# Two units of seven products for q and k of the first half in the input projection of an encoder layer

## The chip, the cores and the metric

The kernel runs on one core of one Trainium2 chip. The metric is the time of one execution on the device in microseconds (us), the median of several runs. A core has TensorE (matrix products, called PE in the profile, its weight loads PEld), VectorE (DVE), ScalarE (ACT), GpSimd (POOL) and SyncE (SP, which here only issues DMAs). Each of them works through its own instructions in the order in which they were written and waits for the others by semaphores.

## The reference

The reference is one layer of an encoder over 256 tokens of width 2048: an input projection, attention and a recurrent block side by side, an output projection, a dense feed-forward part and a gated embedding, each with norms. Only the start is touched here:

```python
hn = rms_norm(h, g_mix_pre[i])
u = hn @ w_in[i]
q, k, v, xr, yg = jnp.split(
    u, [D_ATTN, 2 * D_ATTN, 3 * D_ATTN, 3 * D_ATTN + D_REC], axis=-1)
attn = neighborhood_attention(
    q.reshape(B, S, N_ATTN_HEADS, HEAD_DIM),
    k.reshape(B, S, N_ATTN_HEADS, HEAD_DIM),
    v.reshape(B, S, N_ATTN_HEADS, HEAD_DIM), rpb[i])
rec = rglru_bidirectional(xr, conv_w[i], conv_b[i], w_rg_a[i], b_rg_a[i],
                          w_rg_i[i], b_rg_i[i], lam[i]) * jax.nn.gelu(yg)
```

`w_in` is 2048 x 5120 in float32: q, k, v, x (`xr`) and gate (`yg`) of 1024 columns each.

## The kernel before

**Precision.** Every float32 operand is split into a high part, rounded by ScalarE's cast, and a low part, the difference that VectorE takes. A product is three matmuls, high by high, low by high and high by low, added up in PSUM.

**Tiles.** The feature matrix `hT` has 16 blocks of 128 features by 256 tokens. A weight tile holds two feature blocks (a row-block pair, `[P, 2, N]`, 512 KB) by 512 columns. It is loaded by SP into one of four buffers `wr` (L612), cast to `wh` (L700), its low part goes to `wl` (L716), each with four buffers. Its products (L758) are 2 blocks x 2 halves of the tokens x 3 = 12 matmuls of 512 columns. A chunk is 512 columns: eight tiles, added up in two PSUM banks. There are eight banks: four `acc`, which the chunks use, and four `sm` for small work such as transposes, gate products and scores.

**Order.** A `Plan` runs while the program is written. It holds a clock for each engine and a model of durations, takes the segments of products in order as the main line of TensorE, and puts the side work (generators that yield what they need) between them by readiness and lateness. What it writes is a fixed order for each engine. On the chip an engine waits where its next instruction isn't ready.

**The input projection** runs its ten chunks in the order `x0 v0 q0 k0 x1 q1 k1 v1 g0 g1` (L1493). x0 and v0 take turns tile by tile, all but the last two of each (`turns`, `apart=2`), then come q0's eight tiles, k0's eight and so on. So tiles 0 to 13 are x0's and v0's in turns with x0's last two, 14 and 15 v0's last two, 16 to 23 q0's, 24 to 31 k0's.

**What lies beside it.** While the first tiles are multiplied, `xT` is loaded and turned into the high and low parts of `hT` (L331, L333), block by block. The rows of `x` are loaded a second time as `xn` (L965) ahead of tiles 10 to 13; ScalarE squares them (L995) and the norm `rstd_x` comes from the sums. A chunk's accumulators are scaled by `rstd_x` when they are evacuated (L1112, or L1411 and L1415 for v). x's evacuation starts the transposes, the convolution and the recurrent units (`rec_unit`), q's and k's a turn of blocks by VectorE (L353) and by small DMAs through the single tiles `ev` and `sq`.

**Units of seven.** The feed-forward part and the last gate already multiply some row-block pairs in another way. With two chunks side by side, a row-block pair is a 2 x 2 problem: two token halves, two feature blocks, two column blocks. Seven products of sums and differences do for eight. `Group` holds two such chunks. `four_products` makes four of the seven, the first into empty accumulators, `made_of_four` turns these into the running sums (two copies by ScalarE, four steps by VectorE on PSUM), and `two_products` and `one_product` add the other three onto these sums. The weights for it are swapped between the two tiles on the host (`SWAPPED`), so that the sums `Q0+Q1`, `Q0+Q1+R1` and `Q1+R1` are three adds (L641, L643, L647); the last operand is the second one plus a block that GpSimd's queue adds by an accumulating DMA (`added`, L669). The features need four sums and differences for each pair, made by `sums_of` (L869, L876) and split like any operand.

Of the kernel before, what the change touches and what calls it, by code (L numbers as in the profile page):

```python
# [44 lines left out]
PLE_KS = (0, 2)  # L45
BEGIN = (6, 7)
# [5 lines left out]
def seven_ks(f):  # L52
# [13 lines left out]
    (lambda c: (("w_ple_gate", c), ("w_ple_gate", c + 1)), (2,), PLE_KS),  # L66
]
# [187 lines left out]
def layer(ctx: ExitStack, tc: tile.TileContext, a: dict, out: bass.AP):  # L255
# [211 lines left out]
    class Group:  # L467
# [23 lines left out]
        def two(self, j):  # L491
            i = len(tiles)
            tiles.append(None)
            self.twos[j] = i
            lower[self.own[j] + 1] = -1
            segs.append((two_products, self, j, i))
# [77 lines left out]
    def load_stream():  # L574
        for i, tl in enumerate(tiles):
# [3 lines left out]
            w, k, n0 = tl  # L579
            if min(fours) <= i < i_ple:  # L580
                if i in lower:
                    yield (ev_spilled, ev_half_spilled, ev_unmerged)[(0, 0, 1, 2, 2)[lower[i]]]
                yield dma(ISSUE, take=raw_kind(i))
                t = lower_tile(lower[i]) if i in lower else raw_tile(i)
                nc.sync.dma_start(t, a[w][n0 // N, k // 2])
                plan.now += COST["landing"]
                if i in ev_load:
                    loaded[i] = t
                    done(ev_load[i])
                else:  # L590
                    raws[i] = t
                    done(ev_raw[i, 2])
                continue
# [27 lines left out]
    def sum_stream():  # L621

        for i in sorted(fours):
# [26 lines left out]
            done(ev_raw[two, 2])  # L650

# [54 lines left out]
    def lo_stream():  # L706
        last_one = max(f[1] for f in ffn_fours().values())
        for i in range(len(tiles)):
# [16 lines left out]
            if i in fours:  # L725
                plan.add(last_sum(i), plan.now, -2 * SOON)

# [74 lines left out]
    def made_of_four(group):  # L802
# [49 lines left out]
    def sums_of(lhs, kx, hi, lo):  # L852
# [7 lines left out]
        kind = "mid" if lhs is hP or kx == 6 else "T4"  # L860
        for j in range(2):
            h, l = lhs.at[kx + j]
            yield dve(S, take=None if j else kind)
            if not j and kind == "mid":
# [107 lines left out]
    for i in range(2 * NT):  # L972
        extra_loads.setdefault((10 + i, 0), []).append(load_xn(i))
# [75 lines left out]

    def open_p1():  # L1050
        t1["hs"], t1["rec_hi"] = big(0, "hs", F32), big(1, "rec_hi")
# [14 lines left out]
        for n in ("qh", "ql", "kh", "kl"):  # L1066
            t1[n] = p1.tile([P, HB, S], F32R, name=n)
        for n in ("vh", "vl"):
            t1[n] = p1.tile([P, NT, N], F32R, name=n)
        t1["pp"] = p1.tile([P, 2, NT, 2, KEYS], F32R, name="pp")  # L1070
# [6 lines left out]
        nc.gpsimd.memset(ssr, 0.0)  # L1077

# [20 lines left out]
    def second_tiles():  # L1099
        plan.reach(ev_x)  # L1100
        t1["rec_lo"], t1["attnT"] = big(2, "rec_lo"), big(3, "attnT", F32)
        mixT.blocks(t1["rec_hi"], t1["rec_lo"], 8, NB)
# [392 lines left out]
    first = []  # L1495
    for n, c in enumerate(ORDER.split()):
        (n0, post), half = CHUNKS[c[0]], int(c[1])
        ch = Chunk(post(half), (open_p1, second_tiles)[n] if n < 2 else None)
        if n < 2:
            first.append((ch, "w_in", n0 + half * N))  # L1500
# [751 lines left out]
    for i in range(min(fours), max(f[1] for f in fours.values() if f[4] is hF.ev_sums)):  # L2252
        if i % (W_BUFS + MORE_W) < MORE_W:
            more_w[i] = i % (W_BUFS + MORE_W)
    places = list(RING)
    for n, i in enumerate(sorted(lower)):
        lower[i] = next(j for j in places if j < 3 or n < len(lower) - 4)
        places.remove(lower[i])
        places.append(lower[i])
    first_slot = {i: n % 2 for n, i in enumerate(sorted(fours))}  # L2260
# [27 lines left out]
    soonest = min(fours)  # L2288
    plan.add(load_stream(), late=lambda: (
# [8 lines left out]
    plan.add(norm_x())  # L2298
    plan.add(decay(), 30.0)
# [108 lines left out]
```

## Time and profile before

| | |
|---|---|
| median of 3 runs | 1139.56 us (1138.49 to 1139.64) |
| the profiled execution | 1138.81 us |
| its span, first to last instruction | 1137.0 us |
| mean granted TensorE clock | 0.998 |
| TensorE matmuls | 5140 |
| DMA | 269.54 MB, 237 GB/s on average |

The profile is one execution. Its views name engine, source line, operation and the tiles `out<-in`; a group's row gives busy time, the mean of one instruction in ns, and the engine's idle time just before with what ended it. In timelines the first two numbers are the start and the duration in us. A matmul's own duration overlaps with that of its neighbours, since they are pipelined; the distance from one start to the next is what it costs.

### The profile page before, as it was taken

To read this page: it belongs to the slowest core of one execution; us is meant where nothing else is said; L and a number is where in the kernel's file an instruction comes from. 1 tells how busy PE (TensorE), PEld (TensorE's weight loads), DVE (VectorE), ACT (ScalarE), POOL (GpSimd) and SP (SyncE) were. 2 spreads that over 40 slices of the span, in tenths; PEclk is the share of its full clock that TensorE was granted. 3 is DMA by queue.
4 is the path that set the end of the run, shared out by engine and by line. 5 is a ranking of instruction groups with operands and counts; after the bars stand their busy time and mean duration, and the time that the engine had idled before them with its cause. 6 is when DMAs were issued, how large, how long until landed. Compare 5 with 4: busy or idle time off the path is not lost.

```text
span 1137.0 us, 15223 instructions
## 1 busy us (share of the span) xinstructions
PE 1127.5 (99%) x5140; PEld 938.2 (83%) x5140; DVE 962.1 (85%) x1250; ACT 741.0 (65%) x994; POOL 154.5 (14%) x245
## 2 busy tenths in 40 slices
PE   9999999999999999999999999999999999999997
PEld 8888888888888888888888888888888888888886
DVE  6768787788469998899998889999989988888986
ACT  6776788876448566566566656666565664676674
POOL 0000000000000032232011043132121223200200
PEclk9999999999999999999999999999999999999999
DMA  8867566565686986887887777897887788967862
GB/s 311 303 193 219 173 183 187 166 201 181 206 302 184 344 254 226 234 259 222 277 285 232 240 222 216 249 269 235 271 275 280 233 242 255 305 208 271 269 198 101
DMA packets 110686, 269.54 MB, mean 237 GB/s; under 512 B 36432, under 2 KB 42576, under 8 KB 109200
## 3 DMA queue, kind: packets, MB, share of 16 engines
q1 hardware_dynamic: 95568, 242.60, 64.0%
q0 software_dynamic: 14752, 25.84, 11.1%
q8 instruction: 40, 0.66, 0.2%
q14 instruction: 38, 0.31, 0.1%
q10 hardware_dynamic: 288, 0.14, 0.0%
HBM read 250.70 MB, written 9.44 MB: 229 GB/s over the span
## 4 chain that ended last, share of the span: by engine, by line
PE 96%; DVE 1%; ACT 1%; DMA 1%; issue 0%; SPq 0%; DVEq 0%; POOL 0%; ACTq 0%; POOLq 0%
PE acc L758 69%; PE acc L769 8%; PE acc L768 8%; PE acc L767 8%; PE tr L344 1%; DVE wl L716 0%; DMA sq<-ev 0%; PE half L2119 0%; PE acc L2119 0%; PE warm L2305 0%; PE pg L391 0%; PE pg L392 0%; PE pg L393 0%; ACT wh L700 0%; PE po L1435 0%
## 5 line engine op out<-in xcount | busy, mean ns | idle before, releaser
L716 DVE TENSOR_TENSOR wl<-wr,wh 128x1024 fp32r<-128x1024 f32 (+1 forms) x295 | 352.9, 1210 | 77.8 <-ACT wh L700 72.4
L700 ACT CAST wh<-wr 128x1024 fp32r<-128x1024 f32 (+1 forms) x295 | 304.9, 1042 | 136.8 <-PE acc L758 84.2
L758 PE MATMUL acc<-wh,hT_mix_hi 128*128 128x512 f32 x376 | 146.6, 390 | 0.0
L758 PE MATMUL acc<-wh,hT_mix_lo 128*128 128x512 f32 x376 | 146.3, 389 | 0.0
L758 PE MATMUL acc<-wl,hT_mix_hi 128*128 128x512 f32 x376 | 146.3, 389 | 0.0
L700 ACT CAST wh<-ple 128x1024 fp32r<-128x1024 f32 (+1 forms) x75 | 76.0, 1018 | 82.2 <-DVE ple L643 54.6
L363 POOL DMA_DIRECT2D mT<-mid x164 | 96.8, 636 | 238.3 <-DVE mid L353 117.6
L758 PE MATMUL acc<-wl,hT_hi 128*128 128x512 f32 x320 | 124.6, 390 | 0.0
L758 PE MATMUL acc<-wh,hT_hi 128*128 128x512 f32 x316 | 124.5, 394 | 0.0
L758 PE MATMUL acc<-wh,hT_lo 128*128 128x512 f32 x316 | 123.2, 390 | 0.0
L669 POOL DMA_DIRECT2D ple<-in_w_ffn_up x32 | 28.7, 897 | 539.7 <-DVE ple L643 386.3
L716 DVE TENSOR_TENSOR wl<-ple,wh 128x1024 fp32r<-128x1024 f32 (+1 forms) x75 | 88.0, 1177 | 9.3 <-ACT wh L700 9.3
L758 PEld LDWEIGHTS acc<-wl,hT_mix_hi 128*128 128x128 f32 x376 | 70.6, 188 | 14.7 <-DVE wl L716 0.2
L758 PEld LDWEIGHTS acc<-wh,hT_mix_hi 128*128 128x128 f32 x376 | 70.6, 188 | 14.6
L758 PEld LDWEIGHTS acc<-wh,hT_mix_lo 128*128 128x128 f32 x376 | 70.6, 188 | 14.6
L758 PEld LDWEIGHTS acc<-wl,hT_hi 128*128 128x128 f32 x320 | 60.1, 188 | 13.1 <-DVE wl L716 0.2
L758 PEld LDWEIGHTS acc<-wh,hT_lo 128*128 128x128 f32 x316 | 59.4, 188 | 11.6
L758 PEld LDWEIGHTS acc<-wh,hT_hi 128*128 128x128 f32 x316 | 59.4, 188 | 11.4
L758 PE MATMUL acc<-w,hT_mix_hi 128*128 128x512 f32 x144 | 47.3, 389 | 0.0
L716 DVE TENSOR_TENSOR wl<-lower,wh 128x1024 fp32r<-128x1024 f32 x35 | 42.4, 1215 | 3.1 <-ACT wh L700 3.1
L700 ACT CAST wh<-lower 128x1024 fp32r<-128x1024 f32 x35 | 36.6, 1052 | 10.7 <-PE acc L758 6.8
L758 PE MATMUL acc<-wh,hT_ffn_hi 128*128 128x512 f32 x96 | 37.8, 393 | 0.4 <-ACT hT_ffn_hi L331 0.4
(472 smaller groups left out, 2536.6 us busy)
## 6 DMA issues: line engine op xcount, KB each, us to landing
wr<-in_w_in SPq DMA_DIRECT2D x77, 512.0 KB, 4.5
wr<-in_w_ffn_gate SPq DMA_DIRECT2D x70, 512.0 KB, 5.6
wr<-in_w_ffn_down SPq DMA_DIRECT2D x54, 512.0 KB, 6.0
wr<-in_w_ffn_up SPq DMA_DIRECT2D x50, 512.0 KB, 5.0
wr<-in_w_out SPq DMA_DIRECT2D x32, 512.0 KB, 4.4
wr<-in_w_ple_gate SPq DMA_DIRECT2D x30, 512.0 KB, 4.7
lower<-in_w_ffn_up SPq DMA_DIRECT2D x27, 512.0 KB, 6.4
third<-in_w_ffn_gate SPq DMA_DIRECT2D x18, 512.0 KB, 5.7
```

The source lines that it names most:

```text
L344: nc.tensor.transpose(tr[:, b, t * P : (t + 1) * P], e[:, t, sl], ident)
L363: (nc.gpsimd if i in pool else nc.sync).dma_start(dst[32 * j : 32 * j + 32, :, :, i, :], src[32 * i : 32 * i + 32, :, :, j, :],)
L669: nc.gpsimd.dma_start(dst, src, accum_op=ALU.add)
L700: nc.scalar.copy(his[i][:, 0 : src.shape[1], :] if n == 2 else his[i][:, j, :], src)
L716: nc.vector.tensor_tensor(out=los[i][:, m, :], in0=src, in1=f32(his[i][:, m, :]), op=ALU.subtract)
L758: nc.tensor.matmul(accs[t], x[:, sl], w[:, j, :], start=st and m == 0, stop=sp and m == 2, **group)
L767: nc.tensor.matmul(dst, x[0], wh, start=start, stop=False, skip_group_check=seeded)
L768: nc.tensor.matmul(dst, x[1], wh, start=False, stop=False, skip_group_check=seeded)
L769: nc.tensor.matmul(dst, x[0], wl, start=False, stop=stop, skip_group_check=seeded)
```

## The change

q0 and k0 become a `Group` side by side. The row-block pairs 0 and 2 of both (`IN_KS`) are units of seven, the other six pairs stay ordinary tiles. The four products of the first unit stand before the sixth turn of x0 and v0, those of the second after it (`IN_AT`). Then come the last two tiles of x0 and of v0, a pair of q and k tiles, two products of the first unit, a pair, the other three products of both units, and then the last four tiles of q0 and of k0 (`apart=4`).

By tiles: 10 and 11 are the four products of the first unit, 12 and 13 x0 and v0, 14 and 15 the four products of the second unit, 16 and 17 x0's last, 18 and 19 v0's last, 20 and 21 a pair of q and k, 22 two products, 23 and 24 a pair, 25 to 27 two, one and one product, 28 to 31 q0's last, 32 to 35 k0's last.

x0 and v0 get `sm` banks, so that q0 and k0 can have all four `acc` banks at once. The sums of the weights go into tiles of the later q, k, probability and `sq` buffers, the feature sums into `at0`, a new tile `sums_more` and v's buffer; these buffers are opened for their own use later (`open_v`, `open_qk`). `in_sums` makes the feature sums, `in_sum_stream` the weight sums, `in_last_sum` the accumulating load. The loads of `xn` move from ahead of tiles 10 to 13 to ahead of tiles 17 to 20 of the new order.

```diff
+IN_KS = (0, 2)
+IN_AT = (5, 6)
...
+    (lambda c: (("w_in", c), ("w_in", c + 2)), (0,), IN_KS),
...
+            if i in in_load:
+                for kb, f in extra_loads.get((i, 0), ()):
+                    yield dma(kb)
+                    f()
+                j, second = in_load[i]
+                yield dma(512, take=None if second else "wr")
+                loaded[i] = in_rows[j] if second else raw_tile(i)
+                nc.sync.dma_start(loaded[i], a[w][n0 // N, k // 2])
+                done(ev_load[i])
+                continue
...
+    def in_sum_stream():
+
+        for j, i in enumerate(into.own):
+            yield ev_load[i]
+            yield ev_load[i + 1]
+            Q, R, both = loaded.pop(i), loaded.pop(i + 1), in_both[j]
+            yield dve(3 * N)
+            nc.vector.tensor_tensor(out=both[:, 0, :], in0=Q[:, 0, :], in1=Q[:, 1, :], op=ALU.add)
+            nc.vector.tensor_tensor(out=both[:, 1, :], in0=both[:, 0, :], in1=R[:, 1, :], op=ALU.add)
+            nc.vector.tensor_tensor(out=Q[:, 1, :], in0=Q[:, 1, :], in1=R[:, 1, :], op=ALU.add)
+            raws[i] = both
...
+    def in_last_sum(j):
+        late, last = into.last[j][:2]
+        there = Event()
+        yield from added(in_both[j][:, 1, :], late[:, 0, :], there)
+        yield there
+        raws[last] = in_both[j][:, 1:2, :]
+        done(ev_raw[last, 2])
...
+    def in_sums():
+        more = t1["pool"].tile([P, 2, N], F32R, name="sums_more")
+        pairs = [[x.rearrange("p k s -> p (k s)") for x in at0], (more[:, 0, :], more[:, 1, :])]
...
+            p = pairs[n]
+            yield from sums_of(hT, kx, *p, t1["here"])
...
-        yield ev_rf
-        yield act(N)
-        u, v = (t2["pool"].tile([P, N], F32, tag="junk", name="u", bufs=2) for _ in range(2))
+        if group.lhs is hT:
+            u, v = (t1["ig"][:, n, :, :].rearrange("p c s -> p (c s)") for n in range(2))
+            yield act(N)
...
-        extra_loads.setdefault((10 + i, 0), []).append(load_xn(i))
+        extra_loads.setdefault((17 + i, 0), []).append(load_xn(i))
...
-        ch = Chunk(post(half), (open_p1, second_tiles)[n] if n < 2 else None)
...
-            turns(first, hT, KS, apart=2)
-        elif n > 1:
-            seg(ch, "w_in", n0 + half * N, hT, KS, after=start_biases if n == 3 else None)
+        ch = Chunk(post(half), {0: open_hs, 1: open_v, 2: open_qk, 3: second_tiles}.get(n), slot="sm" if n < 2 else "acc")
...
+            into = Group([made_of[m] for m in ORDER.split()[2:4]], hT, KS, IN_KS, apart=4)
+            into.own, into.twos, into.last = [], {}, {}
+            m = len(KS) - 2
+            for i, k in enumerate(KS[:m]):
+                for j, b in enumerate(IN_AT):
+                    if i == b:
+                        into.four(j)
+                for d, w, o in first:
+                    seg(d, w, o, hT, [k], i == 0, False)
+            for j, b in enumerate(IN_AT):
+                if b >= m:
+                    into.four(j)
+            for d, w, o in first:
+                seg(d, w, o, hT, KS[m:], first=False)
+            steps = list(('0', '1ab'))
+            m = len(into.rest) - into.apart
+            for i in range(m):
+                into.pair(i)
...
+            for d, w, o in into.chunks if into.apart else ():
+                seg(d, w, o, hT, into.rest[m:], first=False)
+        elif n > 3:
+            seg(*made_of[c], hT, KS)
...
+    plan.add(in_sums(), 17.0, late=-LATE)
+    plan.add(in_sum_stream(), late=-LATE)
```

More of the change, by code (lines that the diff above doesn't have):

```diff
@@ L726, in lo_stream @@
                 plan.add(last_sum(i), plan.now, -2 * SOON)
+            if i in into.own:
+                plan.add(in_last_sum(into.own.index(i)), plan.now)
     MM = 0.2263
@@ L850, in one_product, with sums_of @@
         spent(i)
[L852 removed]
+    def sums_of(lhs, kx, hi, lo, here=None):
         lhs.sums[kx] = {
@@ L859, in sums_of @@
         yield lhs.ev[kx + 1]
-        kind = "mid" if lhs is hP or kx == 6 else "T4"
+        kind = None if here is not None else "mid" if lhs is hP or kx == 6 else "T4"
         for j in range(2):
@@ L863, in sums_of @@
             yield dve(S, take=None if j else kind)
-            if not j and kind == "mid":
+            if not j and not kind:
+                e, f = here[:, 0, :], here[:, 1, :]
+            elif not j and kind == "mid":
                 at_ = mid_tile()
@@ L2259, in layer @@
         places.append(lower[i])
+    in_load = {i + n: (j, n) for j, i in enumerate(into.own) for n in range(2)}
+    for i in in_load:
+        ev_load[i] = Event()
+    for j, i in enumerate(into.own):
+        gives[i] = gives[into.twos[j]] = gives[into.last[j][1]] = "x"
     first_slot = {i: n % 2 for n, i in enumerate(sorted(fours))}
```

61 lines of the change are left out of this document (49 added, 12 removed).

## The prediction

> **What bounds the kernel now.** I began with the page: busy times, then the chain of work that ended last.
>
> ```profile
> span 1137.0 us, 15223 instructions
> PE 1127.5 (99%) x5140; PEld 938.2 (83%) x5140; DVE 962.1 (85%) x1250; ACT 741.0 (65%) x994; POOL 154.5 (14%) x245
> ...
> PE 96%; DVE 1%; ACT 1%; DMA 1%; issue 0%; SPq 0%; DVEq 0%; POOL 0%; ACTq 0%; POOLq 0%
> ```
>
> The chain runs through TensorE for 96% of the span. The view of waits says how much of the rest is TensorE standing still; these are all its rows for the whole kernel.
>
> ```profile
> PE final L2206 <- ACT diag L2204: 2.5, 1, 2.5
> PE warm L2305 <- POOL ones L309: 1.1, 1, 1.1
> PE acc L758 <- ACT hT_ffn_hi L331: 0.4, 1, 0.4
> PE sc L391 <- DVE pp L327: 0.3, 1, 0.3
> ```
>
> That is 4.3 us in all, and only the 0.3 lies in the input projection. So time is won by issuing fewer matmuls and lost by any new wait. The chain in order of time gives the price of a matmul (start, us, what):
>
> ```profile
> 8.22 39.98 PE acc L758 x176
> ...
> 71.10 29.05 PE acc L758 x128
> ```
> ```profile
> 388.28 0.23 PE acc L767
> ...
> 393.78 0.23 PE acc L758
> ```
>
> 39.98/176 = 0.2272 us in an ordinary tile of the head, 29.05/128 = 0.2270 later. In the units of seven that the FFN already has, 24 matmuls lie between 388.28 and 393.78: 0.229 each. The 0.39 us that a single matmul shows elsewhere is its length in the pipeline and isn't used.
>
> The Trainium skill (Perfetto Trace Analysis, Identifying the Most-Contended Engine) calls matmul busy time a bad measure and judges TensorE by the busy share of its weight loads, here 83%. Read so, 17% would be free and six pairs fewer would give 1.13 us, 6 x the mean weight load of the row below. The gapless stretch above speaks for 0.2272 each: 0.188/0.227 is 83% too, so that share is what a full TensorE shows here.
>
> ```profile
> L758 PEld LDWEIGHTS acc<-wh,hT_hi 128*128 128x128 f32 x316 | 59.4, 188 | 11.4
> ```
>
> **What the change removes.** One row-block pair of q0 and k0 takes two tiles now: 2 tiles x 2 row blocks x 2 token tiles x 3 splits = 24 matmuls. As a unit of seven it takes 7 x 3 = 21. Two units: 6 matmuls, 6 x 0.2272 = **1.36 us** off TensorE, 0.12% of the span. Nothing else on TensorE changes in number.
>
> **What it adds, and when it is due.** The head is where the answer lies. Stages of 10 us (PE, PEld, DVE, ACT, POOL busy, clock, DMA share, GB/s):
>
> ```profile
> 10.00:20.00 10.00, 10.00 (x46) 8.13 (x45) 8.26 (x12) 6.92 (x11) 0.00 (x0) 1.00 0.98 370
> 20.00:30.00 10.00, 10.00 (x46) 8.29 (x45) 6.93 (x12) 7.74 (x13) 0.00 (x0) 1.00 0.96 344
> 30.00:40.00 10.00, 10.00 (x46) 8.29 (x45) 5.23 (x7) 8.67 (x13) 0.00 (x0) 1.00 0.93 349
> 40.00:50.00 10.00, 10.00 (x48) 8.28 (x47) 8.78 (x28) 8.29 (x12) 0.00 (x0) 1.00 0.84 274
> 50.00:60.00 10.00, 10.00 (x48) 8.25 (x47) 8.88 (x18) 6.97 (x10) 0.00 (x0) 1.00 0.58 170
> 60.00:70.00 10.00, 10.00 (x54) 8.57 (x53) 6.16 (x7) 6.02 (x8) 0.00 (x0) 1.00 0.75 227
> 70.00:80.00 10.00, 10.00 (x50) 8.45 (x49) 6.61 (x7) 8.64 (x14) 0.00 (x0) 1.00 0.66 202
> 80.00:90.00 10.00, 10.00 (x45) 8.26 (x44) 6.00 (x8) 8.81 (x14) 0.00 (x0) 1.00 0.78 218
> 90.00:100.00 10.00, 10.00 (x46) 8.27 (x45) 9.86 (x18) 5.73 (x8) 0.00 (x0) 1.00 0.69 194
> ```
>
> Up to 40 us the DMA engines are full; VectorE has room from 20 to 40 and from 60 to 90, and none from 90 to 100. Tile 1 starts on TensorE at 8.51 (first row below), a tile lasts 12 x 0.2272 = 2.73 us, so tile 10, the first unit after the change, is due at 8.51 + 9 x 2.73 = 33.05. Its low parts are wanted after two matmuls, at 33.5. The second unit is due one unit (2.73) and two tiles later, at 41.2, its low parts at 41.7.
>
> ```profile
> 8.51 0.39 PE L758 MATMUL acc<-wh,hT_hi 128*128 128x512 f32 x1
> ```
> ```profile
> 19.85 0.42 SPq L965 DMA_DIRECT2D xn<-in_x  x1
> 20.38 0.38 SPq L612 DMA_DIRECT2D wr<-in_w_in  x1
> 20.80 0.50 SPq L965 DMA_DIRECT2D xn<-in_x  x1
> ```
> ```profile
> 30.04 1.05 ACT L700 CAST wh<-wr 128x1024 fp32r<-128x1024 f32 x1 [0.22 <-DMA wr<-in_w_in]
> ```
> ```profile
> 28.09 1.22 DVE L716 TENSOR_TENSOR wl<-wr,wh 128x1024 fp32r<-128x1024 f32 x1
> 31.12 1.23 DVE L716 TENSOR_TENSOR wl<-wr,wh 128x1024 fp32r<-128x1024 f32 x1 [1.81 <-ACT wh L700]
> ```
>
> Now xn, tile 10 and xn again are issued from 19.85 on, and tile 10's cast starts at 30.04, the moment it lands. Afterwards tile 10 (Q) and tile 11 (R) take these places: as many bytes before the second of them as now before tile 10, so R lands at about 30. Then come one add (the other needs only Q), the cast and the difference: 30.0 + 0.69 + 1.05 + 1.22 + 0.2 for hand-overs = 33.2 against 33.5. It fits by 0.3 us if VectorE and ScalarE are free at 30. VectorE was: it waited 1.81 us before 31.12. The prices of what is put before that:
>
> ```profile
> L716 DVE TENSOR_TENSOR wl<-wr,wh 128x1024 fp32r<-128x1024 f32 x18 | 21.9, 1222 | 8.0 <-ACT wh L700 8.0
> ```
> ```profile
> 60.70 3.49 DVE L716 TENSOR_TENSOR wl<-wr,wh 128x1024 fp32r<-128x1024 f32 x3
> ```
> ```profile
> L641 DVE TENSOR_TENSOR ple<-wr 128x512 f32<-128x512 f32 x42 | 28.8, 686 | 0.0
> L823 DVE TENSOR_TENSOR acc<-acc,u 128x512 f32<-128x512 f32 x17 | 11.9, 699 | 0.5
> L876 DVE TENSOR_TENSOR mid<-mid 128x128 f32<-128x128 f32 x12 | 3.2, 289 | 0.0
> L869 DVE TENSOR_TENSOR ple<-hT_mix_hi,hT_mix_lo 128x256 f32<-128x256 f32 x6 | 2.4, 421 | 0.0
> ```
> ```profile
> L816 ACT COPY u<-acc 128x512 f32<-128x512 f32 x17 | 9.9, 581 | 10.7 <-PE acc L769 10.7
> ```
>
> Per unit: three weight sums 3 x 0.686 = 2.06; feature sums 2 x 0.421 + 4 x 0.289 + one 512-wide difference 0.69 = 2.69; together 4.75, for both units 9.5 us of VectorE. From 20 to 41.7 it must do what it did until 40 (6.93 + 5.23 = 12.2), 9.5, and tile 14's difference (1.22), which now comes after 40: 22.9 us in 21.7. Neighbouring instructions overlap by some 0.08 us (an estimate: three differences from 60.70 on in 3.49 us, against 3 x 1.222 = 3.67), which takes 1.6 off some 20 added ones: 21.3. So VectorE is filled to between 98% and 105%.
>
> The wait that this puts before a unit is bounded by nothing on one side, and on the other by 2.4 us: all of one unit's feature sums (2.69) ahead of the weight sums, less the 0.3 of room. From 20 to 30 VectorE was free for 3.07 us, more than one unit's 2.69, and those sums need only the first blocks of hT. So I take a value near the lower end, **0.6 us** for both units together; a late first unit also moves the second one's due time.
>
> ScalarE gets two 512-wide casts more before 41.7 and loses the four squares of xn there (next part): no cost. The combination that turns the products into running sums is two copies of 0.58 and four VectorE steps of 0.69, 3.9 us in series at most. It starts when the second unit ends (44) and is wanted when x0 and v0 have had their last two tiles each (4 x 2.73 = 10.9 us): hidden; without that cover it would cost 3.9. The weight pieces to be split grow from 4 to 7 halves a unit, 6 halves in all, some 3.7 us of VectorE and 3.2 of ScalarE, mostly between 55 and 75, where VectorE was free for 3.8 of 10 us: hidden, and if not, a rival below.
>
> **The accumulating loads** are two of 256 KB on GpSimd's queue, which is empty after its first 10 us (0.00 in the table).
>
> ```profile
> ple<-in_w_ffn_up POOLq DMA_DIRECT2D x12, 256.0 KB, 4.7
> ```
> ```profile
> L965 SPq DMA_DIRECT2D xn<-in_x x4: 422/490/558, 19.9 to 26.7; - x4
> ...
> DMA to landing us min/median/max: 8.8/10.0/10.9
> ```
>
> They start when a unit's first tile has been split (33 and 42) and are wanted after 68: 4.7 us behind 25, no cost. The Trainium skill (DMA: Bandwidth & Descriptors, Issuing engines are not separate DMA queues) says that DMAs of all issuers interleave on the same 16 engines, so a free queue doesn't mean a free path. At 349 GB/s one takes 0.75 us; by that rule the second unit's last load could land 0.75 later and the sum would be 0.75 worse. The DMA share of 0.93 agrees that there is little room, but no row shows such a load in the head.
>
> **The loads of xn move** from ahead of tiles 10 to 13 to ahead of tiles 17 to 20, behind the units' loads on SP's queue. They wait there for the buffers of tiles 11 to 16, the last until about 43, and land 5 to 11 us later, so the norm is ready at 51 to 57, where x0's evacuation now runs at 45:
>
> ```profile
> 45.32 1.26 ACT L1112 ACTIVATE ev<-acc,rstd_x 128x512 f32<-128x512 f32 x2
> ```
>
> x0 then ends at 33.05 + 4 x 2.73 + 2 x 2.73 = 49.4, so its evacuation waits 2 to 8 us. Queued behind it are x0's transposes and the recurrent units, but no product: x0 and v0 lie in the small banks, q0 and k0 have the four large ones. Cost on TensorE: nothing, while the recurrent work comes 6 to 12 us later. q0 ends some 11 us before k0 instead of 22; x1 opens in q0's banks 11 us after q0's end, and an evacuation takes 1.3.
>
> **Sum.** -1.36 + 0.6 = -0.76 us on this execution's 1138.81 (span 1137.0 and 1.8 around it): 1138.05. The median of the runs shown is 0.75 above that execution, so the forecast is 1139.56 - 0.76 = **1138.8**.
>
> **The rivals.** *All of the gain stays*: VectorE's gaps take the sums and no unit waits: 1139.56 - 1.36 = **1138.2**. For it: 3.07 us free against 2.69, and the room of 0.3. Against: gaps are waits for ScalarE (1.81 before 31.12) and don't come when they suit.
>
> *The units wait as long as they can*: 2.4 us, and 0.75 for the load in the way: -1.36 + 2.4 + 0.75 = +1.8, **1141.3**. For it: VectorE at 105% by plain durations. Against: all feature sums would have to come in the last moment.
>
> *Slower, by a backlog of VectorE at 90 to 105 us*: the late recurrent work and the added 3.7 + 2.8 = 6.5 us (halves, combination) pile up where VectorE is at 9.86 of 10. From 20 to 100 it was free for 21.6 us; the change asks for 9.5 + 6.5 = 16.0, so 5.6 are left. If waits between engines eat more than these, differences of weights come late and TensorE waits; from 1.4 us of it on the kernel is slower than before, and with all 6.5 it is 1139.56 - 1.36 + 6.5 = **1144.7**. Against: 11.2 us are free from 60 to 90, and the recurrent work isn't due soon.
>
> That the units don't save what they say is no rival: the count of matmuls follows from the code, and 0.229 a matmul in such units would change 42 matmuls by 0.1 us.
>
> **Chances.** Forecast 0.45; all stays 0.30; units wait in full 0.12; backlog 0.13. What a measurement here can tell from no change is about 0.2%, 2.3 us: below 1137.3 or above 1141.8. Faster than that takes the full gain and a lucky 0.9 us of the 1.15 us by which the three runs differ: 0.05. Slower takes most of the backlog: 0.12. The rest, 0.83, is no change. The range is 1137.1 (full gain on the lowest run, 1138.49) to 1141.8, which takes in the full waits and leaves out the upper part of the backlog.
>
> **What would show it.** Right: 5134 matmuls; small waits of TensorE at the units' first tiles near 33 and 41 us, on the difference (VectorE) or the cast, 0.6 us together; x0's evacuation at 51 or later; none at the combination. Wrong: waits beyond 1 us there, a wait at 85 to 110 us, or a stretch after 260 us whose length changes by as much as the head's.

## The result, and the profile after

| | before | after |
|---|---|---|
| median of 6 runs | 1138.61 us (1137.79 to 1139.64) | 1147.97 us (1147.35 to 1156.19) |
| ratio, 95% interval | | 1.0098 [1.0078, 1.0119] |
| profiled execution | 1138.81 us | 1151.9 us |
| its span | 1137.0 us | 1150.1 us |
| mean granted TensorE clock | 0.998 | 0.994 |

The change makes the kernel slower by 9.4 us, 0.98%, where 1138.8 us and no change were forecast. The page of the changed kernel, its span, busy times and the chain that ended last:

```profile
span 1150.1 us, 15274 instructions
PE 1132.5 (98%) x5134; PEld 939.2 (82%) x5134; DVE 975.3 (85%) x1278; ACT 743.5 (65%) x1000; POOL 156.2 (14%) x247
...
PE 92%; DVE 3%; ACT 2%; DMA 1%; issue 1%; SPq 0%; DVEq 0%; POOL 0%; ACTq 0%; POOLq 0%
```

The six matmuls are gone (5134). But VectorE, ScalarE and DMA now hold 6% of the chain, where they held 3%. TensorE's waits (us in total, times, longest), all rows:

```profile
PE acc L810 <- DVE wl L766: 7.8, 5, 3.0
PE final L2307 <- ACT diag L2305: 2.5, 1, 2.5
PE warm L2415 <- POOL ones L312: 1.1, 1, 1.1
PE tr L347 <- ACT ev L1186: 0.8, 1, 0.8
PE acc L810 <- ACT hT_ffn_hi L334: 0.4, 1, 0.4
```

The second, third and last row were there before. New are five waits of products for a low part `wl`, and one of a transpose. The view of stages says where (us, then busy time of PE, PEld, DVE, ACT, POOL, granted clock, DMA share, GB/s), first after, then before:

```profile
20.00:40.00 20.00, 18.49 (x81) 14.67 (x80) 17.74 (x34) 11.67 (x20) 0.99 (x1) 1.00 0.79 253
40.00:60.00 20.00, 16.60 (x64) 12.46 (x63) 15.48 (x33) 15.30 (x22) 0.86 (x1) 0.91 0.89 305
100.00:120.00 20.00, 16.98 (x78) 13.85 (x77) 15.02 (x22) 9.39 (x12) 0.00 (x0) 0.99 0.68 185
120.00:140.00 20.00, 20.00 (x92) 16.96 (x92) 12.41 (x13) 17.92 (x30) 0.00 (x0) 0.92 0.84 228
```
```profile
20.00:40.00 20.00, 20.00 (x90) 16.57 (x89) 12.16 (x19) 16.41 (x26) 0.00 (x0) 1.00 0.95 347
40.00:60.00 20.00, 20.00 (x94) 16.53 (x93) 17.66 (x44) 15.26 (x21) 0.00 (x0) 1.00 0.71 222
```

TensorE stands for 1.5, 3.4 and 3.0 us in three stages, and in two stages, 40 to 60 and 120 to 140, the granted clock is down: 20 x 0.09 and 20 x 0.08, 3.4 us more. That is 11.3; less the 1.36 gained, about 10 of the 13.1 us by which the spans differ. Taken from the start of each matmul of 512 columns to the next start, what goes beyond 0.2272 us by more than 0.15 adds up to 12.7 us after and 1.1 before, the smaller excesses to 5.2 and 3.5: 11.6 + 1.7 - 1.4 = 11.9, and the transpose's wait of 0.8 comes on top.

In the first stage VectorE was busy for 17.74 of 20 us, so it was idle for 2.3 us while TensorE waited 1.5 us for it. Over the stretch of the prediction's balance, 20 to 41.7 us, it was busy for 19.44 of 21.7 us, 90%:

```profile
20.00:41.70 21.70, 20.19 (x88) 15.99 (x87) 19.44 (x36) 13.13 (x21) 0.99 (x1) 1.00 0.80 253
```

Its timeline (start, us, what, and the idle time before it with what ended that) shows how:

```profile
23.75 1.02 DVE L934 TENSOR_TENSOR here<-here 128x128 f32<-128x128 f32 x4
26.42 1.68 DVE L336 SCALAR_TENSOR_TENSOR hT_lo<-xs,g_first,hT_hi 128x256 fp32r<-128x256 f32 x4 [1.66 <-ACT hT_hi L334]
28.02 1.22 DVE L766 TENSOR_TENSOR wl<-wr,wh 128x1024 fp32r<-128x1024 f32 x1
29.16 0.69 DVE L330 TENSOR_TENSOR at_lo<-here,at_hi 128x512 fp32r<-128x512 f32 x1
29.76 0.69 DVE L673 TENSOR_TENSOR both_kl<-wr 128x512 f32<-128x512 f32 x1
30.48 0.69 DVE L674 TENSOR_TENSOR both_kl<-both_kl,rows_qh 128x512 f32<-128x512 f32 x1
31.09 0.68 DVE L675 TENSOR_TENSOR wr<-wr,rows_qh 128x512 f32<-128x512 f32 x1
31.69 1.22 DVE L766 TENSOR_TENSOR wl<-wr,wh 128x1024 fp32r<-128x1024 f32 x1
```

The low part of tile 8 (28.02) stands behind the last four blocks of `hT`, for which VectorE waits 1.66 us, and that of tile 9 (31.69) behind the split of the first feature sums and the first unit's three weight sums. Their casts were long done, at 23.1 and 25.6:

```profile
22.08 1.04 ACT L750 CAST wh<-wr 128x1024 fp32r<-128x1024 f32 x1
24.56 1.05 ACT L750 CAST wh<-wr 128x1024 fp32r<-128x1024 f32 x1 [1.45 <-DMA wr<-in_w_in]
```

TensorE waits 0.9 and 0.7 us for these two. In the second stage the same happens on two engines, ScalarE and then VectorE:

```profile
44.53 1.06 ACT L1053 ACTIVATE xn<-xn 128x1024 f32<-128x1024 f32 x1 [3.07 <-DMA xn<-in_x]
...
45.58 1.04 ACT L750 CAST wh<-wr 128x1024 fp32r<-128x1024 f32 x1
47.09 1.06 ACT L1053 ACTIVATE xn<-xn 128x1024 f32<-128x1024 f32 x1 [0.47 <-DMA xn<-in_x]
...
48.15 1.04 ACT L750 CAST wh<-wr 128x1024 fp32r<-128x1024 f32 x1
```
```profile
49.69 0.69 DVE L874 TENSOR_TENSOR ig<-ig,acc 128x512 f32<-128x512 f32 x1 [1.52 <-ACT ig L872]
...
51.82 0.69 DVE L881 TENSOR_TENSOR acc<-acc,ig 128x512 f32<-128x512 f32 x1
52.41 2.35 DVE L766 TENSOR_TENSOR wl<-wr,wh 128x1024 fp32r<-128x1024 f32 x2
```

The casts of tiles 16 and 17 (45.58, 48.15) queue behind squares that wait for xn; then the low part of tile 17 (52.41) queues behind the four steps of the combination, the first of which waits 1.52 us itself. TensorE waits 0.5 us at tile 16 and 2.7 at tile 17. In the third stage VectorE's low part at 116.98 stands behind that of the recurrent gates' weights, whose cast waits for a load:

```profile
107.69 0.39 SPq L1215 DMA_DIRECT2D av<-in_w_rg_a  x1
```
```profile
114.76 1.05 ACT L328 CAST gh<-av 128x1024 fp32r<-128x1024 f32 x1 [4.00 <-DMA av<-in_w_rg_i]
```
```profile
115.84 1.22 DVE L330 TENSOR_TENSOR gl<-av,gh 128x1024 fp32r<-128x1024 f32 x1 [4.28 <-ACT gh L328]
116.98 1.22 DVE L766 TENSOR_TENSOR wl<-wr,wh 128x1024 fp32r<-128x1024 f32 x1
```

These gates' loads stand on SP's queue behind six small copies of q's turn and go out from 107.69. The five waits have one form: an instruction that itself waits stands in an engine's queue ahead of one that TensorE needs, next to it or with ready work between the two. The transpose's wait, 0.8 us at 195, wasn't followed.

### The profile page after: what moved, and what is told of

The parts are those of the page before. It is cut to its first block, busy times and chain, and to the rows that moved or that the text cites. A ratio compares the mean times of both kernels' runs of the same rounds, so it can differ in the third digit from the quotient of the medians.

```text
span 1150.1 us, 15274 instructions
## 1 busy us (share of the span) xinstructions
PE 1132.5 (98%) x5134; PEld 939.2 (82%) x5134; DVE 975.3 (85%) x1278; ACT 743.5 (65%) x1000; POOL 156.2 (14%) x247
## 3 DMA queue, kind: packets, MB, share of 16 engines
q0 software_dynamic: 15040, 26.36, 11.3%
## 4 chain that ended last, share of the span: by engine, by line
PE 92%; DVE 3%; ACT 2%; DMA 1%; issue 1%; SPq 0%; DVEq 0%; POOL 0%; ACTq 0%; POOLq 0%
PE acc L810 65%; PE acc L820 8%; PE acc L819 8%; PE acc L821 8%; PE tr L347 1%; DVE wl L766 1%; DMA xn<-in_x 1%; DMA sq<-ev 1%; ACT wh L750 1%; SPq L366 0%; PE half L2220 0%; PE acc L2220 0%; PE warm L2415 0%; PE pg L395 0%; PE pg L396 0%
## 5 line engine op out<-in xcount | busy, mean ns | idle before, releaser
L810 PE MATMUL acc<-wl,hT_hi 128*128 128x512 f32 x304 | 120.1, 396 | 7.9 <-DVE wl L766 7.8
L810 PE MATMUL acc<-wh,hT_hi 128*128 128x512 f32 x300 | 119.8, 399 | 0.1
L810 PE MATMUL acc<-wh,hT_lo 128*128 128x512 f32 x300 | 117.9, 393 | 0.0
L810 PEld LDWEIGHTS acc<-wh,hT_hi 128*128 128x128 f32 x300 | 57.1, 190 | 11.3 <-ACT wh L750 0.6
L810 PEld LDWEIGHTS acc<-wh,hT_lo 128*128 128x128 f32 x300 | 57.0, 190 | 11.0
```

The source lines that it names most:

```text
L810: nc.tensor.matmul(accs[t], x[:, sl], w[:, j, :], start=st and m == 0, stop=sp and m == 2, **group)
```

## The experiments

The first seven keep the order of the changed kernel but for what is named. What they ask is which late instruction makes which wait, and whether the places in the queues or VectorE's amount of work is behind it; each expectation names its own theories. A miss is a time outside what the theory of the order of the queues forecast. All times are medians; the kernel before was 1138.2 to 1138.8 us beside them. Waits are those of one profiled execution each.

**1. The squares don't wait for xn.** xn is still loaded, but the squares read half of xT's data, so the norm is one of other numbers.

```diff
-            nc.scalar.activation(v, v, AF.Square, accum_out=ss[:, t, c : c + 1])
+            o = xs_half[0].rearrange("p k s -> p (k s)")[:, c * DA : (c + 1) * DA]
+            nc.scalar.activation(o, o, AF.Square, accum_out=ss[:, t, c : c + 1])
```

> The changed kernel, but ScalarE's four squares for the norm of x read a tile of xT that landed long before, instead of xn; xn is still loaded at the same places and the order of every engine stays. The norm is therefore that of other numbers. Theory A (engines stand in a fixed order, and ScalarE waits for xn with the casts of tiles 16 and 17 behind it): the waits of TensorE at 47.9 (0.5 us) and 53.7 (2.7 us) go, the time falls by 3 to 4 us, to about 1144.5. Rival B (VectorE has too much to do up to 55 us): the squares are not VectorE's work, so its low parts stay late and at least 2 us of these waits remain. Rival C (DMA bandwidth makes tiles 16 and 17 late): the casts still start after 45, waits stay.

1145.14 us (1143.75 to 1147.8), 1.0063 [1.0048, 1.0078]. Its waits for low parts:

```profile
PE acc L810 <- DVE wl L766: 3.3, 4, 1.6
```

The wait at tile 16 is gone, that at tile 17 is 1.6 where it was 2.7, since the low part still follows the combination. Some 3 us go with the late squares, not all of the loss. More goes than the waits behind them: the wait at 118 is 0.3 here (at 113), though nothing about its loads was edited, and no stage of the first 280 us has a lower clock; x0's transposes now wait 1.2 us at 59.

**2. The gates' loads on GpSimd's queue**, past SP's.

```diff
-                nc.sync.dma_start(
+                nc.gpsimd.dma_start(
```

> The changed kernel, but the loads of the recurrent gates' weights are issued on GpSimd's queue, which is empty then, instead of on SP's, where they stand behind the small loads that turn q. Theory A: at 105 they go out at once, the gates' high part starts about 3 us earlier than 114.8, the low part of tile 40 behind it is in time, the wait of TensorE at 118.3 (3.0 us) shrinks to below 0.7, the time falls by 2.5 to 3 us, to about 1145. Rival B (a backlog of VectorE): the wait stays at 2 us or more, since VectorE has as much to do.

1146.9 us (1146.14 to 1147.58), 1.0075 [1.006, 1.0091].

```profile
PE acc L810 <- DVE wl L766: 5.1, 4, 2.7
```

One of the five waits is gone, the one of 3.0 us at 118, so moving the loads is enough to remove it. That their place on SP's queue alone makes it isn't shown: it is 0.3 us in 1 and absent in 5 and 6, where the loads keep this place but go out from 103.7, 105.6 and 105.4. The time moves by 1.1 us, less than the two intervals can tell apart.

**3. The last blocks of hT don't wait.** Blocks 12 to 15 are made from earlier blocks of xT, so their features are others.

```diff
-                    hT_hi[:, b, :], hT_lo[:, b, :], xs[k][:, j, :], g_first[:, b : b + 1]
+                    hT_hi[:, b, :], hT_lo[:, b, :], xs[k - 2 * (b >= 12)][:, j, :], g_first[:, b : b + 1]
```

> The changed kernel, but the last four blocks of hT (12 to 15) are made from xT blocks 8 to 11, which land earlier; the products of these blocks are therefore those of other features. All orders stay. Theory A: VectorE no longer waits for the last xT load at 24.8 to 26.4 with the low part of tile 8 behind it: TensorE's wait at 29.3 (0.9 us) goes and that at 33.0 (0.7) shrinks, the time falls by 1.0 to 1.6 us. Rival B (VectorE full from 20 to 42 us): 1.6 us of idle time filled moves all its work forward, the waits go too, but then VectorE shows no idle time before 33; theory A expects it to stand idle for the loads of tiles 10 and 11 instead.

1149.05 us (1146.67 to 1150.26), 1.0092 [1.0077, 1.0107]: a miss. The group of blocks starts at the same time, now behind the cast of tile 9, which waits for a weight buffer that TensorE has to free. Two waits lay side by side, and the removed one only hid the other.

**4. The three together.**

> The three edits together (squares from an early tile, gates' loads on GpSimd's queue, last hT blocks from earlier xT blocks; norm and products are of other numbers). Theory A: 3.3 + 3.0 + 1.6 = 7.9 us of waits go, about 1140, and 1.4 to 2 us above the full gain of 1137.2 remain (one wait at a transpose near 195 us, 0.8 us, and small ones). Rival B: VectorE's work is the same, so the waits come back at the next tiles and the time stays above 1143.

1147.43 us (1147.04 to 1147.76), 1.0079 [1.0062, 1.0096]: a miss, and 2.3 us more than with the squares alone. TensorE still waits 2.2 us at tile 17: its cast, free of the squares, now waits for a buffer, and the combination is as much in the way as before.

**5. The first two squares later**, put off until the third, behind the casts of tiles 16 to 18.

```diff
...
+            held.append((v, ss[:, t, c : c + 1]))
+            while i > 1 and held:
+                v, s = held.pop(0)
+                nc.scalar.activation(v, v, AF.Square, accum_out=s)
```

> The changed kernel with the first two of ScalarE's squares of xn put behind the casts of tiles 16, 17 and 18, next to the third; nothing else moves. Theory A, as e1 left it (two things stand ahead of the low part of tile 17, the squares on ScalarE and the four steps of the combination on VectorE): like e1, the wait at tile 16 (0.5 us) goes and that at tile 17 falls from 2.7 to between 1.5 and 2.3; about 1145. If the squares were all: no wait there. If the time of e1 came from its other operands and not from the wait for xn: no change, 1148.

1147.69 us (1146.69 to 1150.33), 1.0082 [1.0067, 1.0097]: a miss, and the time that the third theory, no change, had named. The profile says why it isn't borne out: the wait at tile 16 goes and tile 17 keeps 1.7 us, about as in 1. But tile 8 waits 2.1 us where it waited 0.9, since the cast of tile 9, ahead of the last blocks of `hT`, waits 3.3 us for its load, and the transposes behind x0's evacuation wait 1.6 us at 61.

**6. Four low parts first.** The low parts of tiles 8, 9, 16 and 17 are put right behind that of the tile before, ahead of blocks, sums and combination.

```diff
+    def low(i):
+        if i in FIRST and i in his and i not in lowered and (i - 1 in lowered):
+            nc.vector.tensor_tensor(out=los[i], in0=raws[i], in1=f32(his[i]), op=ALU.subtract)
+            lowered.add(i)
+            low(i + 1)
...
```

> The changed kernel with the low parts of tiles 8, 9, 16 and 17 put on VectorE right behind the low part of the tile before, as soon as their casts are written: ahead of the last blocks of hT, of the sums and of the combination. VectorE does the same amount of work, every other order stays. Theory A (order): the waits at tiles 8 and 9 (0.9 and 0.7) go, that at tile 17 falls from 2.7 to 0.5 or less, since its cast ends at 49.2; the wait at tile 16 stays; together 3.5 to 5 us, about 1143.5. Rival B (VectorE full): what is put back comes late in turn: the first unit's low parts are late by 1 us or more, or the combination makes TensorE wait at 60; the time stays above 1146.

1145.57 us (1143.95 to 1148.39), 1.006 [1.004, 1.008]. The waits at tiles 8, 9 and 17 are gone with the same work on VectorE; that at tile 16 is 0.4. New ones of 0.2 to 0.7 us stand at tiles 10, 11 and 18, and transposes wait 2.4 us for their evacuations, 1.6 of it for x0's at 59. The time lies between the two theories: above 1143.5, below the 1146 of a full VectorE.

**7. All orders at once**: four low parts first, the squares later, the gates' loads on GpSimd's queue.

> Both orders and the gates' loads on GpSimd's queue: the changed kernel with three edits, the same numbers computed. Theory A: the waits at tiles 8, 9, 16, 17 and 40 go, 7 to 8 us, and with them the halved clock that follows the longest; 1138.5 to 1140, no slower than before by more than 0.2%. If it is below 1138.2, the two units gain. Rival B: above 1143, waits of 1 us and more at other tiles of the first 120 us.

1148.83 us (1147.7 to 1149.54), 1.0088 [1.0072, 1.0103]: a miss; rival B's time. ScalarE's timeline at the squares, then TensorE's wait:

```profile
54.88 1.06 ACT L1069 ACTIVATE xn<-xn 128x1024 f32<-128x1024 f32 x1 [2.07 <-DMA xn<-in_x]
...
55.94 1.98 ACT L758 CAST wh<-wr 128x1024 fp32r<-128x1024 f32 x2
```
```profile
PE acc L822 <- ACT wh L758: 2.7, 1, 2.7
```

Put off, the squares hold up the cast of tile 19 in place of those of 16 and 17. Whatever comes behind them waits until xn has landed.

**8. xn early.** Its loads go out from GpSimd's queue behind the low parts of tiles 7 and 8; an element written by VectorE holds each back until then.

```diff
...
+                for x in XN_AT.pop(i, ()):
+                    t, c = x // 2, slice(x % 2 * DA, (x % 2 + 1) * DA)
+                    nc.vector.memset(xn[t][:, c][:, 0:1], 0.0)
+                    nc.gpsimd.dma_start(xn[t][:, c], a["x"][t * P : (t + 1) * P, c])
...
```

> Result unchanged; only the four loads of xn go out from GpSimd's queue, the first two behind the low part of tile 7 and the last two behind that of tile 8 (some 24 to 30 us, where they went out at 37 to 45 from SP's queue); every other instruction keeps its order. Theory A (the squares and x0's transposes wait for xn, and the late landing is a cause of its own): the wait at tile 16 (0.7 us) and the transposes' waits at 57 to 60 us go, the wait at tile 17 falls from 2.9 us to about 1.7 (the combination's four steps ahead of its low part stay), so the halved clock behind it goes; tiles 8 and 9 and the gates' 3.2 us stay: 1143.5 to 1146. Theory B (landing is set by the DMA engines being full, whatever the issue): the squares wait as long, or the weights of tiles 10 to 17 land later and TensorE waits for those: 1146 to 1150.

1147.73 us (1147.56 to 1148.02), 1.0077 [1.0062, 1.0092]: theory A's figures fail, theory B's hold. No square waits for xn any more, but the loads that xn went past come later, and VectorE waits for them:

```profile
42.32 0.69 DVE L674 TENSOR_TENSOR both_pp<-both_pp,rows_ql 128x512 f32<-128x512 f32 x1 [1.82 <-DMA rows_ql<-in_w_in]
...
43.53 1.22 DVE L766 TENSOR_TENSOR wl<-wr,wh 128x1024 fp32r<-128x1024 f32 x1
```

The low part of tile 13 (43.53) stands behind the second unit's sums, and TensorE waits 2.8 us for it (the second unit's cast starts at 43.1, at 39.5 in the changed kernel). At tile 8 it waits 1.8 us, 0.9 in the changed kernel.

**9. xn early, four low parts first, gates' loads on GpSimd's queue.**

> xn's loads early as in the run before, with the low parts of tiles 8, 9, 16 and 17 ahead of the sums, blocks and combination, and the gates' loads on GpSimd's queue. Theory A (three orders and one late load make up the loss): the waits at tiles 8, 9, 16, 17, at the transposes at 57 to 60 and at the gates all go; what is left are a few tenths at tiles 10, 11 and 18: 1139 to 1141. Theory B (taking one wait away makes another, since VectorE and ScalarE are full there): 2 to 4 us of waits come up at tiles 10 to 19: 1142 to 1146.

1144.5 us (1140.86 to 1145.8), 1.0043 [1.0027, 1.0059], the lowest median of all forms (14 can't be told from it) and apart from the change itself by its interval. The time is theory B's, that taking one wait away makes another. Two of its stages:

```profile
20.00:40.00 20.00, 19.25 (x84) 15.24 (x82) 18.46 (x37) 11.91 (x20) 3.18 (x5) 1.00 1.00 369
40.00:60.00 20.00, 18.30 (x80) 14.68 (x81) 17.58 (x44) 17.59 (x27) 3.76 (x5) 1.00 0.80 245
```

VectorE gets through more in both stages than in the changed kernel (18.46 and 17.58 us against 17.74 and 15.48), and TensorE stands for 2.5 us, not 4.9. This is the profile of the fastest execution, 1140.86 us; what keeps the others 3.6 to 5 us above it was not seen.

**10. The low parts of tiles 10, 11 and 18 first as well.**

> As the run before, with the low parts of tiles 10, 11 and 18 put right behind the previous tile's too. Theory A: nothing of the first 200 us is left but tenths: 1138 to 1139.5, at or just below the kernel before. Theory B: the low parts put ahead delay the blocks, sums and the combination, and their readers (the units, the next chain's start) wait: 1141 to 1146.

1145.77 us (1144.15 to 1147.86), 1.0061 [1.0048, 1.0073]: a miss, in theory B's range. The waits ahead of 50 us get smaller, but x0's transposes now wait 2.3 us and a later one 1.0.

**11. Only xn's loads late, in the kernel before**: ahead of tiles 14 to 17; the plan is made anew round them.

```diff
-        extra_loads.setdefault((10 + i, 0), []).append(load_xn(i))
+        extra_loads.setdefault((14 + i, 0), []).append(load_xn(i))
```

> The kernel before, with the one edit that xn's four loads stand ahead of the loads of tiles 14 to 17, not 10 to 13; its hand-planned order shifts a little round it, no unit, no sum and no combination is there. Theory A (the late xn is a cause by itself): xn lands after 35 us, the squares and x0's evacuation hold casts and transposes up, TensorE waits 1 to 4 us between 35 and 60: 1140 to 1143. Theory B (the late xn hurts only where VectorE and ScalarE are already full with the units' sums and combination): the squares slide into ScalarE's idle time, no wait over 0.3 us: 1138 to 1139.2.

1138.45 us (1138.28 to 1139.41), 1.0001 [0.9992, 1.0011]: theory B of this run. ScalarE:

```profile
35.28 1.06 ACT L995 ACTIVATE xn<-xn 128x1024 f32<-128x1024 f32 x1 [3.22 <-DMA xn<-in_x]
...
47.47 1.27 ACT L1112 ACTIVATE ev<-acc,rstd_x 128x512 f32<-128x512 f32 x2 [0.23 <-DVE rstd_x L400]
```

Here too a square waits 3.2 us for xn, and x0's evacuation is 2.2 us later, but the plan has its casts far enough ahead and no product waits. An xn that is late by this much costs nothing by itself; in the changed kernel x0's evacuation is 13.6 us later (58.91 against 45.32), and that much wasn't tried here.

**12. xn's loads ahead of tiles 10 to 13 again, in the changed kernel**; the plan is made anew round it.

```diff
-        extra_loads.setdefault((17 + i, 0), []).append(load_xn(i))
+        extra_loads.setdefault((10 + i, 0), []).append(load_xn(i))
```

> The changed kernel with the one edit that xn's loads stand ahead of the loads of tiles 10 to 13 again; the plan is made anew round it. Theory A: xn lands before 40 us, the waits at tiles 16 and 17 and at x0's transposes go with it, those behind the sums and the blocks at tiles 8 and 9 stay or grow, since the loads of the units' rows come later: 1141 to 1144. Theory B (the units' own sums and combination make the loss): 1146 to 1150, with waits of 2 us or more at tiles 8 to 18 and none of them behind a square.

1155.09 us (1154.45 to 1156.52), 1.0149 [1.0132, 1.0166]: both theories miss.

```profile
PE acc L810 <- ACT ev L1186: 6.4, 1, 6.4
```

In 20 to 60 us TensorE is busy for 18.05 + 19.17 us, so it stands for 2.8 us in place of 4.9, as A had it, but the order made anew has one wait of 6.4 us at 263, where an evacuation stands behind attention's splits. The comparison is one of two whole orders, not of one moved load.

**13. The feature sums' additions on GpSimd**, idle there; the products and the split are the same.

```diff
...
-            nc.vector.tensor_tensor(out=dst, in0=x, in1=y, op=ALU.subtract)
+            (nc.vector if here is None else nc.gpsimd).tensor_tensor(out=dst, in0=x, in1=y, op=ALU.subtract)
```

> The changed kernel with the feature sums' additions (twelve steps of the two pairs) on GpSimd, which is idle there, in place of VectorE; their split stays. Theory A (VectorE's amount of work from 20 to 42 us makes the waits): some 4 us of VectorE's time are freed, the wait at tile 9 goes and that at tile 8 shrinks, and all behind comes earlier: 1142 to 1146. Theory B (the place in the queue makes them): the split of the sums now waits on VectorE for the slower GpSimd, the low parts stand behind it as before, TensorE waits 1 to 3 us at tiles 9 to 11: 1146.5 to 1150.

1149.12 us (1147.02 to 1151.18), 1.0091 [1.0075, 1.0107]: theory B's time.

```profile
20.00:40.00 20.00, 18.39 (x80) 14.59 (x79) 15.52 (x22) 11.88 (x20) 4.54 (x5) 1.00 0.80 268
```

VectorE is relieved of 2.2 us in this stage (15.52 against 17.74), idle for 4.5 of 20 us, and TensorE stands as long as before the edit, 0.6 us at tile 8 and 1.1 at tile 9. The low part of tile 8 again stands behind the blocks, for which VectorE waits 1.6 us:

```profile
26.25 1.68 DVE L336 SCALAR_TENSOR_TENSOR hT_lo<-xs,g_first,hT_hi 128x256 fp32r<-128x256 f32 x4 [1.59 <-ACT hT_hi L334]
27.85 1.22 DVE L766 TENSOR_TENSOR wl<-wr,wh 128x1024 fp32r<-128x1024 f32 x1
```

So the amount of work in this stage isn't what makes these two waits.

**14. As 9, with the norm early**: squares behind the casts of tiles 13 to 15, their sum behind the low part of tile 16, the root behind the cast of tile 19.

```diff
...
+                for x in SQ_AT.pop(i, ()):
+                    s, c = x // 2, x % 2
+                    v = xn[s][:, c * DA : (c + 1) * DA]
+                    nc.scalar.activation(v, v, AF.Square, accum_out=ss[:, s, c : c + 1])
+                if i == RT_AT:
+                    nc.scalar.activation(rt, tot, AF.Sqrt, bias=eps, scale=1.0 / D)
...
```

> As e9 (xn early, four low parts ahead, gates' loads on GpSimd's queue), with the squares put behind the casts of tiles 13, 14 and 15, the sum of the squares behind the low part of tile 16 and the root behind the cast of tile 19; all of VectorE's work stays. Theory B (the queues' order makes the waits): the transposes' wait of 1.8 us at 55 to 57 goes, tenths to 1 us stay at tiles 10 to 13: 1138.5 to 1141. Theory A (the amount of work): the waits come up elsewhere, 3 us or more together ahead of 70 us: 1142 to 1146.

1144.66 us (1142.7 to 1146.1), 1.0051 [1.0037, 1.0064]: in the range of theory A, the amount of work, with some 3 us of waits ahead of 70 us as it said. No faster than 9: the cast of tile 19 now waits for its own load, and x0's evacuation behind it comes no earlier.

```profile
52.10 1.05 ACT L758 CAST wh<-wr 128x1024 fp32r<-128x1024 f32 x1 [3.12 <-DMA wr<-in_w_in]
```

**15. 13 and 14 together.**

> e14 and e13's additions on GpSimd together. If both amount and order count, this is the fastest of all: 1137.5 to 1139, waits under 1.5 us ahead of 200 us. If GpSimd's additions come too late for the units or the order was not the cause, 1141 to 1146.

1146.15 us (1144.75 to 1147.12), 1.0062 [1.0049, 1.0076]: a miss for both its branches, 0.15 us above the second. One of the first unit's weight sums is three times as long while GpSimd adds, so the cast of tile 10 is late and TensorE waits 0.8 us for it. VectorE, then GpSimd:

```profile
30.71 2.08 DVE L674 TENSOR_TENSOR both_kl<-both_kl,rows_qh 128x512 f32<-128x512 f32 x1
```
```profile
30.79 1.44 POOL L953 TENSOR_TENSOR here<-hT_hi,hT_lo 128x256 f32<-128x256 f32 x2
```

No form of the change reached the time of before. Taken together: that the order makes the waits at tiles 8, 9 and 17 is shown, since they go with the same work in another order (6) and those at 8 and 9 stay with less work in the same order (13). That the order makes the whole loss isn't. In 7, 9, 10 and 14 the time came out where the theories of full engines had it: as the named waits went, others came up. With VectorE busy for 18.16 to 18.83 of 20 us in 20 to 40 in these four, an order may not have enough room, and no run takes work from VectorE without holding it up elsewhere (13 and 15 make its sums wait for GpSimd).

## Why the prediction was wrong, by its own steps

- **The gain term** was right: six matmuls, 1.36 us, 5134 left.
- **"What it adds, and when it is due"** is the step that failed. It balanced VectorE's work from 20 to 41.7 us against the time there, got 98 to 105% and made 0.6 us of it. Measured are 90% and 4.9 us of TensorE standing in 20 to 60, with 3.0 more at 118. A balance over 20 us says nothing on who stands behind whom. In the changed kernel VectorE had 2.3 us to spare in 20 to 40; with 2.2 us of work less the waits at tiles 8 and 9 were as long (13), and with the same work in another order they were gone (6). Here the order costs: blocks that aren't ready, and sums and combination behind what they wait for, stand ahead of low parts whose inputs are. The waits weren't at the units' first tiles, as the last part of the prediction had it, but at tiles 8, 9, 16 and 17.
- **"ScalarE ... loses the four squares of xn there: no cost"** and **"Cost on TensorE: nothing"** for the moved loads: the squares were followed to x0's evacuation, and "no product" was named as queued behind. The casts of tiles 16 and 17 are queued behind them. The late x0 itself made no wait in the changed kernel, but 1.2 to 2.3 us in 1, 5, 6, 9, 10 and 14, where TensorE came to its transposes earlier. By 1 some 3 us hang on the late squares, by 5, where other waits grew, none; by 11 a lesser lateness costs nothing where the queues around it are otherwise laid.
- **The combination "hidden"**: hidden from those who read it, as said. But the low part of tile 17 stands behind it on VectorE, and TensorE still waits 1.6 us for it when no square is late (1).
- **The rival of a backlog at 90 to 105 us** had the sign and a place not far off: 3.0 us at 118. Its mechanism was another: no lack of VectorE's time, since VectorE stood idle for 4.3 us before the gates' low part, but late loads of the gates' weights, behind q's turn on SP's queue; past that queue the wait is gone (2). The prediction moved the recurrent work later without asking past which queue its DMAs would go.
- **The granted clock** had no term. It took some 3.4 us of the profiled execution, which is 3.9 us above the median. Three executions of 1147.35 to 1147.69 us show 0.998 or 0.999, as before the change, so most of the 9.4 us is there without it.
- The stretch after 260 us didn't change: the view of waits has no new row there, and from the first product that reads `hT_mix` to the end it is 788.7 us, 788.6 before.

Open stays what separates 9's executions from one another and its median from the time before. Each order that was tried took named waits away, and others of 0.2 to 2.7 us came up, most of them behind x0's norm and the weight loads. Whether an order without any exists, or VectorE and ScalarE have too much to do for one, wasn't shown; the nearest is the execution of 1140.86 us.

## What to carry to other kernels

Where engines run fixed queues, cost an added instruction by its place: name what must be ready before it, and which instruction behind it in that queue is the next one the bounding engine needs; the share of busy time can't answer this. Follow a delayed load through each queue that its readers stand in, to the next cast or difference, not only to the next result. Taking one late instruction away helps only if the next one in the same queue isn't late as well.

## What the runs showed of the hardware

A short wait of TensorE can cost more than itself. After the wait of 2.73 us at tile 17 the matmuls go on at full pace for a microsecond, then eight of them start 0.43 us apart, not 0.23 (start, us):

```profile
53.68 0.50 PE L810 MATMUL acc<-wl,hT_hi 128*128 128x512 f32 x1 [2.73 <-DVE wl L766]
54.02 0.39 PE L810 MATMUL acc<-wh,hT_hi 128*128 128x512 f32 x1
...
55.00 0.63 PE L810 MATMUL acc<-wh,hT_lo 128*128 128x512 f32 x1
...
57.56 0.63 PE L810 MATMUL acc<-wh,hT_lo 128*128 128x512 f32 x1
```

From the start at 54.72 to the ninth after it, at 58.36, are 3.64 us, where 9 x 0.2272 = 2.04 would do: some 1.6 us lost. The delay isn't fixed: in 2 the first matmul behind the same wait (2.74 us) is slow already, 0.80 us long against the 0.50 above. Nor does every wait bring it: in 4 one of 2.2 us did (clock 0.91 in 40 to 60), in 5 one of 2.1 us did not (1.00). And it depends on the execution: the changed kernel took 1147.35 to 1147.69 us where the mean clock was 0.998 or 0.999, and 1151.9 and 1156.19 at 0.994, so the clock goes with much of the spread, though these two differ by 4.3 us at one clock. The Trainium skill (TensorE: Matmul & The Clock Gate, What's actually happening) tells of two clock states and of a free-running window of 3413 ns; the stretch at half clock, some 3.4 us, and the differing delays agree. The Trainium skill (TensorE: Matmul & The Clock Gate, Why this matters for your kernels) advises against idle gaps over about 3 us; here 2.7 us were enough, and 2.2 in 4.

GpSimd's additions can slow VectorE's beside them. In 15 a weight sum took 2.08 us while two of GpSimd's ran, against 0.69 in the changed kernel, in rows shown above. GpSimd's two end at 30.79 + 1.44 = 32.23, and VectorE's step ends at 30.71 + 2.08 = 32.79, 0.56 later. The Trainium skill (SBUF — State Buffer, Who interferes with whom) says that a VectorE instruction with two inputs in SBUF contends with a GpSimd instruction that reads SBUF, for ports that one of them holds alone. The step in 15 agrees, but VectorE's began 0.08 us ahead of GpSimd's, so the order of the starts doesn't tell who waits. In 13 weight sums beside GpSimd's additions took only 0.83 to 0.97 us, so the delay is far from fixed.
